# Near attention: the softmax weights are turned once per unit and repeated over the head's rows by DMA through DRAM

## The chip, the core and the metric

The kernel runs on one core of a Trainium2 chip. The metric is the device time of one execution, in microseconds; the profile's own clock, the span from the first to the last instruction, stands beside it. The core has five engines that work through their own instruction queues in order: TensorE (PE in the profile; PEld is its weight load), VectorE (DVE), ScalarE (ACT), GpSimd (POOL) and SyncE (SP, which here only issues DMA). ACT issues DMA too.

## The reference, cut to what matters

One layer of an encoder over 1024 tokens of width 1024. After an input layer norm, one projection makes the queries, keys and values of 24 attention heads (three groups of 8, with dilations 1, 4 and 16), the inputs of a bidirectional gated recurrence of 8 heads, and two merge gates. The change touches the end of the attention. Each group is a softmax over a window, and the three groups' outputs are mixed head by head with a softmax over their log-sum-exps:

```
def dilated_attention(aq, ak, av, slopes):
    for g, (window, dil) in enumerate(ATT_GROUPS):
        o, lse = dilated_group(aq[:, :, g], ak[:, :, g], av[:, :, g], window, dil, slopes[g])
    ...
    w = jax.nn.softmax(jnp.stack(lses), axis=0)
    o = jnp.sum(w[..., None] * jnp.stack(outs), axis=0)
```

Behind it come the output projections of attention and recurrence, the gated sum, two layer norms and a SwiGLU feed-forward layer.

## The kernel before, in words

**Stages.** Phase 1 makes the projection and, in between, the attention and the recurrence. Phase 2 merges them and applies the first norm, phase 3 is the feed-forward layer. Every float32 product is made of three matmuls on a rounded part and the rest ("hi" and "lo"): `mm3` (lines 272 to 274) issues hi x hi, hi x lo, lo x hi. The projection uses Winograd's form of Strassen's product: seven products over blocks of 128 columns, two column groups in turn, each product being 4 x 3 = 12 matmuls of 128x512 (a step, in what follows, is one of these matmuls). A product's weight block is loaded by SP (line 251, tiles `wa`), cut by a CAST on ACT (line 214, `w_hi`) and a subtraction on POOL (line 224, `w_lo`), three products ahead, in four buffers. ACT copies (line 726) and DVE adds (lines 572 to 599) bring the results out of the PSUM tiles `pj`; from there they go to DRAM (`hg..` for the recurrence, `at..` for attention).

**Units.** Between the steps of the projection's stream `phase1` runs side work, one unit at a time, written as a generator that gives way at each `yield`. There are 4 attention units (two of the 8 heads each, j = 0 to 3) in two parts, `att_far` (dilations 4 and 16) and `att_near` (dilation 1), and 8 recurrence heads (`hgrn_side`). A unit's inputs come from DRAM into ten slots of 128x1024 (`slot(n, ...)`), and its PSUM tiles are the four buffers `sd` (`ps_sd`). Behind each of the first three `att_near` stands a recurrence head. Its first t (slot 1) and second t (slot 3), q and hv are loaded by `fetch` (line 780); ACT turns t into the gate tiles fa and fb (lines 1149 to 1155), DVE scans them (line 1162), POOL multiplies t with fb (line 1170) and with their inverses (line 1183), and TensorE turns the result (line 1197). The tile fb of the head's first direction lies in slot 7, where the attention's result `ol` was.

**att_near, part by part.** `far` gives the far groups' result OL (128 rows: 64 for each of the two heads; 1024 tokens along the row) and their negative maxima N12 and sums L12. The scores of each 128 queries are made with the queries on partitions, with maximum, exp and sum (lines 1013 to 1030). Then both weights are worked out as tiles [128 queries, 2 heads, 8 query blocks], W0 for the near group and W12 for the far ones (lines 1035 to 1044). But OL and the near result have the head's rows on partitions and the queries along the row, so the weights must be turned, and each be repeated over the 64 rows of its head. Before, POOL first repeats every weight 64 times along the row (RB, two tiles of 128x1024, line 1048), and TensorE turns the 2 x 8 blocks of 128x128 (`spread`, line 1070), so that the repeated columns become repeated rows. The near weights are copied from PSUM to `near` (line 1075), the far ones stay in two PSUM tiles RL. The scores are turned as well (line 1062, 32 transposes), and 64 small matmuls with V give the near result in the two PSUM tiles O (line 1089). At the end OL = OL x RL + near x O (lines 1094 to 1098), stored by ACT (line 1099).

**What sets the order.** The kernel is built under a scheduler. It estimates each instruction's time, keeps the dependences, gives evacuations of `pj` a head start (`high_priority`), and fixes for each engine one order in which it then issues. The waits that are left are semaphores. Line numbers of the changed kernel are one higher above `att_near` and shift by a few inside it.

Of the kernel before, what the change touches and what calls it, by code (L numbers as in the profile page):

```python
# [10 lines left out]
F32 = mybir.dt.float32  # L11
# [9 lines left out]
T = 1024  # L21
KT = D // 128
HALF = 512
# [56 lines left out]
class Block:  # L80
    evac_ahead = 1000

    def __init__(self, ctx, tc, x, ln_in_g, ln_in_b, w_in, hgrn_lb, hgrn_norm_g, w_att_up, w_hgrn_up,
                 w_o, ln1_g, ln1_b, w_ffn_in, w_ffn_out, ln2_g, ln2_b, tabs, out, dbg=None):
        self.tc, self.nc, self.ctx = tc, tc.nc, ctx
        self.x = x[0]
        self.ln = {"in": (ln_in_g, ln_in_b), "1": (ln1_g[0], ln1_b[0]), "2": (ln2_g[0], ln2_b[0])}
        self.w_in, self.lbw, self.ng = w_in[0], hgrn_lb, hgrn_norm_g[0]
        self.wa, self.wr, self.wo = w_att_up[0], w_hgrn_up[0], w_o[0]
        self.wfi, self.wfo, self.tabs, self.out = w_ffn_in[0], w_ffn_out[0], tabs, out[0]  # L90
        self.dbg = dbg or {}
        nc = self.nc

        self.npj = 0
        self.issued = {}
        self.psum = ctx.enter_context(tc.tile_pool(name="psum", bufs=1, space=PSUM))
        self.cst = ctx.enter_context(tc.tile_pool(name="cst", bufs=1))
        self.tiny = ctx.enter_context(tc.tile_pool(name="tiny", bufs=1))
        self.spare = self.pad(self.cst, CST_PAD)
        self.wpool = self.pool("wp", "right")  # L100
        self.wp = self.wpool.__enter__()
        dram = ctx.enter_context(tc.tile_pool(name="dram", bufs=1, space=DRAM))

        def scratch(name, n):
            if name in self.dbg:
                return [self.dbg[name][i] for i in range(n)]
            return [dram.tile([128, 1024], F32, name=f"{name}{i}") for i in range(n)]

        self.att_d = scratch("att", 4)
        self.rec_d = scratch("rec", 8)  # L110
        self.tg_d = scratch("tg", 16)
        self.n1_d = scratch("n1", 8)
        self.ahs_d = scratch("ahs", 8)
        self.hg_d = [{n: dram.tile([128, T], F32, name=f"hg{h}{n}") for n in ("t0", "t1", "q", "v", "g")}
                     for h in range(8)]
        self.at_d = [{(k, g): dram.tile([128, T], F32, name=f"at{j}{k}{g}") for k in "qkv" for g in range(3)}
                     for j in range(4)]
        self.td = [dram.tile([128, 4, HALF], F32, name=f"td{i}") for i in range(3)]
        self.gd = {p: dram.tile([128, NF // 2, HALF], F32, name=f"gd{p}") for p in range(1, 8)}
        self.consts()  # L120
# [695 lines left out]
    HD = (slice(0, 64), slice(64, 128))  # L816
# [165 lines left out]
    def att_near(self, j, pre):  # L982


        nc, ident, HD, d = self.nc, self.ident, self.HD, self.at_d[j]
        OL, N12, L12 = self.far
# [45 lines left out]
                yield 2  # L1032
        V = self.turned(v.rearrange("p (k d) -> p k d", k=8), lambda kt: v[:, 128 * kt:128 * kt + 128])

        NM, W0, W12 = (self.att_small(n) for n in ("NM", "W0", "W12"))
        nc.vector.tensor_tensor(NM, N0, N12, OP.min)
        for w, n, l in ((W0, N0, L0), (W12, N12, L12)):
            nc.vector.tensor_sub(w, NM, n)
# [4 lines left out]
        for w in (W0, W12):  # L1043
            nc.vector.tensor_mul(w, w, L0)

        RB = [self.slot(1 + i, f"rb{i}", (8, 2, 64)) for i in range(2)]
        for r, w in zip(RB, (W12, W0)):
            nc.gpsimd.tensor_copy(r, w.rearrange("p a t -> p t a")[:, :, :, None].to_broadcast([128, 8, 2, 64]))
        yield 2

        kw = dict(skip_group_check=True)
# [4 lines left out]
        for b in range(4):  # L1056
            for hd in range(2):
                ps = self.ps_sd()
# [4 lines left out]
                self.copied(hd, P[b][:, hd].rearrange("p t c -> p (t c)"), ps)  # L1063
            if b % 2:
                yield b
        def spread(r):
            out = [self.ps_sd(), self.ps_sd()]
            for tt in range(8):
                c = 128 * (tt % 4)
                nc.tensor.transpose(out[tt // 4][:, c:c + 128], r[:, tt].rearrange("p a d -> p (a d)"), ident)  # L1070
            return out

        near = self.slot(2, "near")
        for b, ps in enumerate(spread(RB[1])):
            nc.scalar.copy(near[:, HALF * b:HALF * (b + 1)], ps)
        RL = spread(RB[0])
        O = [self.ps_sd(), self.ps_sd()]
        todo = []
        for kt in range(8):
            c = 128 * (kt % 4)  # L1080

            todo.append((kt, O[kt // 4], c + (64 if kt == 0 else 0), c + 128, kt, 192 if kt == 0 else 128))
            t = kt + 1
# [7 lines left out]
            begun.add(id(o))  # L1091
        cols = ((0, slice(64, 512), slice(0, 448)), (1, slice(0, 512), slice(448, 960)), (0, slice(0, 64), slice(960, 1024)))
        for b, src, dst in cols:
            nc.vector.tensor_mul(OL[:, dst], OL[:, dst], RL[b][:, src])
        for b, src, dst in cols:
            z = slice(HALF * b + src.start, HALF * b + src.stop)
            nc.vector.tensor_mul(near[:, z], near[:, z], O[b][:, src])
# [945 lines left out]
```

## Time and profile before

| | |
|---|---|
| median of 3 runs | 2035.15 us |
| lowest and highest run | 2034.71 and 2042.38 us |
| span of the profiled execution | 2034.2 us (its own device time is not shown beside it) |
| granted TensorE clock, mean | 0.998 |
| TensorE busy | 2005.5 us, 99% |
| DVE, ACT, POOL busy | 1310.3, 961.4 and 1026.6 us (64, 47 and 50%) |
| att_near, the part with `spread`, units 0 to 3 | starts at 344.8, 592.2, 840.6 and 1086.7 us |

The device time holds the span and what lies around it; the median stands 0.95 us above the span. A row of a timeline gives the start, the length in us, the engine, the line, the operation, "written tile <- read tiles", the shape, a count where equal neighbours are merged, and in brackets how long the engine stood idle before it and for whom. Matmuls overlap, so what one costs is read from the distance of starts and not from its length.

### The profile page before, as it was taken

The numbers are of one execution on the slowest core, as the hardware profiler recorded it, in microseconds if no ns is written. First come the engines' busy times: TensorE is split into PE (matmuls) and PEld (weight loads), VectorE is DVE, ScalarE is ACT, GpSimd is POOL, SyncE is SP. The second block draws the span as 40 slices with busy tenths as digits, with TensorE's granted clock in tenths as the row PEclk, the third lists the DMA queues.
The fourth block names the chain that finished last, engine by engine and source line by source line (L and its number), as shares of the span: only waits on it lengthen the run. The fifth ranks groups of instructions, "written<-read, shape, count | busy, mean of one in ns | idle before, by whom it ended". The sixth has DMA issues, their size and how long they took to land. (4 is left out here: it accounts for less than half of the span.)

```text
span 2034.2 us, 31011 instructions
## 1 busy us (share of the span) xinstructions
PE 2005.5 (99%) x11002; PEld 1666.0 (82%) x11002; DVE 1310.3 (64%) x2065; ACT 961.4 (47%) x1980; POOL 1026.6 (50%) x890
## 2 busy tenths in 40 slices
PE   7999999999999999999999999999999999999998
PEld 5788888788888888888888888888788888888886
DVE  7777545884458843778444226557776776767788
ACT  6654455554655535665465433244433333344541
POOL 6656644676446663466545662244765665630000
PEclk9999999999999999999999999999999999999999
DMA  5443533445333453343534477444434443447533
GB/s 160 153 137 120 174 118 109 132 135 171 119 123 125 135 170 104 125 141 125 170 99 149 132 258 234 143 144 141 139 135 140 135 140 130 129 168 288 165 98 126
DMA packets 274430, 296.93 MB, mean 146 GB/s; under 512 B 14113, under 2 KB 207458, under 8 KB 274274
## 3 DMA queue, kind: packets, MB, share of 16 engines
q1 hardware_dynamic: 267968, 273.73, 42.2%
q10 hardware_dynamic: 6306, 21.20, 2.7%
q8 instruction: 87, 1.43, 0.3%
q14 instruction: 69, 0.57, 0.1%
HBM read 200.77 MB, written 94.11 MB: 145 GB/s over the span
## 5 line engine op out<-in xcount | busy, mean ns | idle before, releaser
L224 POOL TENSOR_TENSOR w_lo<-wa,w_hi 128x512 fp32r<-128x512 f32 x272 | 364.4, 1349 | 273.5 <-ACT w_hi L214 235.0
L214 ACT CAST w_hi<-wa 128x512 fp32r<-128x512 f32 x272 | 168.7, 621 | 252.8 <-PE pj L273 151.5
L224 POOL TENSOR_TENSOR w_lo<-wsum,w_hi 128x512 fp32r<-128x512 f32 x88 | 127.9, 1464 | 111.1 <-PE sd L274 60.7
L224 POOL TENSOR_TENSOR w_lo<-f_raw,w_hi 128x512 fp32r<-128x512 f32 x66 | 101.2, 1540 | 51.5 <-ACT w_hi L214 50.3
L210 POOL TENSOR_TENSOR mv<-mv,mhalf 128x1 f32<-128x1 f32 x16 | 12.7, 792 | 221.7 <-DVE mv L209 218.6
L214 ACT CAST w_hi<-wsum 128x512 fp32r<-128x512 f32 x88 | 54.6, 621 | 116.7 <-PE sd L273 108.8
L214 ACT CAST gwsum<-a_raw 128x512 fp32r<-128x512 f32 (+1 forms) x78 | 48.2, 618 | 112.5 <-PE pj L273 54.1
L272 PE MATMUL pj<-xt1hi,w_hi 128*128 128x512 f32 x252 | 99.8, 396 | 0.0
L274 PE MATMUL pj<-xt1hi,w_lo 128*128 128x512 f32 x252 | 98.7, 392 | 0.0
L273 PE MATMUL pj<-xt1lo,w_hi 128*128 128x512 f32 x252 | 98.4, 391 | 0.0
L224 POOL TENSOR_TENSOR w_lo<-ws,w_hi 128x512 fp32r<-128x512 f32 x46 | 64.5, 1406 | 55.1 <-ACT w_hi L214 54.8
L583 DVE TENSOR_TENSOR evh<-wkeep,pj 128x512 f32<-128x512 f32 x45 | 30.8, 685 | 95.3 <-PE pj L274 55.5
L698 POOL TENSOR_TENSOR wa<-wa,wa 128x512 f32<-128x512 f32 x46 | 67.5, 1469 | 48.9 <-DVE wa L697 45.6
L572 DVE TENSOR_TENSOR evh<-wkeep,pj 128x512 f32<-128x512 f32 x66 | 58.0, 882 | 39.7 <-PE pj L274 29.4
L726 ACT COPY wkeep<-pj 128x512 f32<-128x512 f32 x136 | 79.4, 585 | 2.0 <-DVE evh L572 2.0
L274 PE MATMUL pj<-xt2hi,w_lo 128*128 128x512 f32 x192 | 75.8, 395 | 2.5 <-POOL w_lo L224 2.5
L273 PE MATMUL pj<-xt2lo,w_hi 128*128 128x512 f32 x192 | 75.5, 393 | 1.3 <-DVE xt2lo L404 1.3
L272 PE MATMUL pj<-xt2hi,w_hi 128*128 128x512 f32 x192 | 76.0, 396 | 0.7 <-ACT w_hi L214 0.7
L224 DVE TENSOR_TENSOR gwkeep<-a_raw,gwsum 128x512 fp32r<-128x512 f32 (+1 forms) x78 | 53.1, 680 | 36.5 <-ACT gwsum L214 33.7
L272 PE MATMUL pj<-xb11hi,w_hi 128*128 128x512 f32 x192 | 76.0, 398 | 0.4 <-DVE evh L583 0.4
L272 PE MATMUL pj<-xt4hi,w_hi 128*128 128x512 f32 x192 | 76.3, 397 | 0.0
L273 PE MATMUL pj<-xb11lo,w_hi 128*128 128x512 f32 x192 | 75.5, 394 | 0.0
(449 smaller groups left out, 6584.1 us busy)
## 6 DMA issues: line engine op xcount, KB each, us to landing
wa<-in_w_in_dram SPq DMA_DIRECT2D x184, 256.0 KB, 3.3
f_raw<-in_w_ffn_in_dram SPq DMA_DIRECT2D x44, 512.0 KB, 4.2
a_raw<-gd SPq DMA_DIRECT2D x30, 512.0 KB, 3.7
gd<-fc SPq DMA_DIRECT2D x44, 256.0 KB, 2.0
gd<-fs SPq DMA_DIRECT2D x33, 256.0 KB, 2.6
tg<-evh SPq DMA_DIRECT2D x32, 256.0 KB, 2.4
tg<-tg SPq DMA_DIRECT2D x16, 512.0 KB, 5.7
y<-ahs SPq DMA_DIRECT2D x16, 512.0 KB, 6.9
```

What stands on the lines that cost most here:

```text
L210: nc.gpsimd.tensor_tensor(mv[:, 2:3], mv[:, 2:3], self.mhalf[:, 0:1], OP.pow)
L214: ins = nc.scalar.copy(hi, src) if eng_hi == "act" else nc.vector.tensor_copy(hi, src)
L224: ins = e.tensor_sub(lo, src, hi.bitcast(F32))
L272: nc.tensor.matmul(ps, whi, xhi, start=first, stop=False, **kw)
L273: nc.tensor.matmul(ps, whi, xlo, start=False, stop=False, **kw)
L274: self.product = nc.tensor.matmul(ps, wlo, xhi, start=False, stop=last, **kw).ins.name
L572: self.left(nc.vector.tensor_tensor(o, self.order_src(add, g, kind), s, OP.add))
L583: self.left(nc.vector.tensor_add(t, add, ps))
L698: nc.gpsimd.tensor_sub(a["a21"], a["a22"], a["a11"])
L726: nc.scalar.copy(t, ps)
```

## The change

The two weights lie in one tile WW [128, 2 weights, 2 heads, 8 blocks]. One TensorE transpose makes of it 32 rows (weight, head, block) of 128 queries. ACT copies them to SBUF and stores them to a DRAM tile of 16 KB per unit. A head's 8 rows of one weight are, read on end, its 1024 queries; four DMA loads of SP (each 64 rows x 4 KB, all from the same 4 KB of DRAM) repeat them over the head's 64 rows in `near` (slot 2) and RL (slot 1). RL now is an SBUF tile, not two of PSUM, and the two POOL copies, 16 transposes and two ACT copies per unit are gone.

```diff
@@ att_near
+        WW = self.smt.tile([128, 2, 2, 8], F32, name="WW", tag="WW", bufs=1)
+        W0, W12 = WW[:, 0], WW[:, 1]
...
-        RB = [self.slot(1 + i, f"rb{i}", (8, 2, 64)) for i in range(2)]
-        for r, w in zip(RB, (W12, W0)):
-            nc.gpsimd.tensor_copy(r, w.rearrange("p a t -> p t a")[:, :, :, None].to_broadcast([128, 8, 2, 64]))
+        ps = self.ps_sd()
+        nc.tensor.transpose(ps[0:32, 0:128], WW.rearrange("p w a t -> p (w a t)"), ident)
+        wr = self.sm.tile([128, 128], F32, name="wrow", tag="xtmp", bufs=1)[0:32, :]
+        nc.scalar.copy(wr, ps[0:32, 0:128])
+        nc.scalar.dma_start(self.w_d[j], wr)
+        near, RL = self.slot(2, "near"), self.slot(1, "rl")
+        for w, t in enumerate((near, RL)):
+            for hd in range(2):
+                src = self.w_d[j][16 * w + 8 * hd:16 * w + 8 * hd + 8, :].rearrange("a b -> (a b)")
+                nc.sync.dma_start(t[HD[hd]], src[None, :].to_broadcast([64, T]))
         yield 2
...
-        def spread(r):
-            out = [self.ps_sd(), self.ps_sd()]
-            for tt in range(8):
-                c = 128 * (tt % 4)
-                nc.tensor.transpose(out[tt // 4][:, c:c + 128], r[:, tt].rearrange("p a d -> p (a d)"), ident)
-            return out
-
-        near = self.slot(2, "near")
-        for b, ps in enumerate(spread(RB[1])):
-            nc.scalar.copy(near[:, HALF * b:HALF * (b + 1)], ps)
-        RL = spread(RB[0])
...
-            nc.vector.tensor_mul(OL[:, dst], OL[:, dst], RL[b][:, src])
+            nc.vector.tensor_mul(OL[:, dst], OL[:, dst], RL[:, HALF * b + src.start:HALF * b + src.stop])
```

The scheduler's order changes with it. TensorE in unit 0, first before, where the weights (`rb_`) are turned between two steps of the projection:

```order
L274 MATMUL pj<-xt3hi,w_lo 128x512
L1070 MATMUL sd<-tabs_sb,rb_3471 128x128 x8
L1070 MATMUL sd<-tabs_sb,rb_3470 128x128 x8
L272 MATMUL pj<-xt3hi,w_hi 128x512
L273 MATMUL pj<-xt3lo,w_hi 128x512
```

And after at the same place, where the products with V now stand (before, they came 20 steps of the projection later):

```order
L275 MATMUL pj<-xt3hi,w_lo 128x512
L1088 MATMUL sd<-p_3287,v_3263 64x64 x2
L1088 MATMUL sd<-p_3287,v_3263 64x128 x4
L1088 MATMUL sd<-p_3311,v_3263 64x128 x8
L1088 MATMUL sd<-p_3374,v_3263 64x128 x8
L1088 MATMUL sd<-p_3390,v_3263 64x128 x8
L1088 MATMUL sd<-p_3287,v_3263 64x64 x2
L273 MATMUL pj<-xt3hi,w_hi 128x512
```

The new transpose stands three steps of the projection later than the first score transposes stood before, ahead of those, which are cut into groups of 12, 4, 12 and 4:

```order
L275 MATMUL pj<-xt2hi,w_lo 128x512
L1050 MATMUL sd<-tabs_sb,WW 32x128
L1072 MATMUL sd<-tabs_sb,p_3287 128x128 x8
L1072 MATMUL sd<-tabs_sb,p_3311 128x128 x4
L273 MATMUL pj<-xt2hi,w_hi 128x512
```

SP behind the weights of unit 0, first before, then after; `t_3713` and `t_3700` are the first t of the next recurrence head, `t_3717` and `t_3704` the second:

```order
L251 DMA wa_3608<-in_w_in_dram 128x4x128
L251 DMA wa_3628<-in_w_in_dram 128x4x128
L585 DMA hg3t_131<-evh 128x512
L780 DMA t_3713<-hg2t_125 128x1024
L251 DMA wa_3723<-in_w_in_dram 128x4x128
L573 DMA hg3v<-evh 128x512
L251 DMA wa_3744<-in_w_in_dram 128x4x128
L780 DMA hv<-hg2v 128x1024
L780 DMA q<-hg2q 128x1024
L780 DMA t_3717<-hg2t_126 128x1024
```

```order
L1058 DMA near<-wd_191 64x1024 x2
L1058 DMA rl<-wd_191 64x1024 x2
L252 DMA wa_3598<-in_w_in_dram 128x4x128
L781 DMA t_3700<-hg2t_125 128x1024
L252 DMA wa_3618<-in_w_in_dram 128x4x128
L252 DMA wa_3638<-in_w_in_dram 128x4x128
L586 DMA hg3t_131<-evh 128x512
L252 DMA wa_3710<-in_w_in_dram 128x4x128
L781 DMA hv<-hg2v 128x1024
L781 DMA q<-hg2q 128x1024
L781 DMA t_3704<-hg2t_126 128x1024
```

The first t moved from behind the store of `hg3t_131` to ahead of it and of two weight loads. ACT at the head behind unit 0, before and after; the conversions of `wa_3404` and `wa_3425` before are those of `wa_3408` and `wa_3429` after:

```order
L1149 ACTIVATE fa<-t_3713,gb,ga 128x8x63
L214 CAST w_hi<-wa_3404 128x512
L584 ACTIVATE evh<-evh 128x512
L1099 DMA att_71<-ol 128x1024
L214 CAST w_hi<-wa_3425 128x512
L1154 ACTIVATE fa<-t_3717,gb,ga 128x8x63
L1155 ACTIVATE fb<-t_3717,gb,ga 128x8x65
```

```order
L1098 DMA att_71<-ol 128x1024
L1153 ACTIVATE fa<-t_3704,gb,ga 128x8x63
L1154 ACTIVATE fb<-t_3704,gb,ga 128x8x65
L215 CAST w_hi<-wa_3408 128x512
L1149 ACTIVATE fb<-t_3700,gb,ga 128x8x65
L1156 ACTIVATE t_3704<-t_3704,ga,gna 128x1024
L585 ACTIVATE evh<-evh 128x512
L1156 ACTIVATE t_3700<-t_3700,ga,gna 128x1024
L215 CAST w_hi<-wa_3429 128x512
```

Both conversions moved from ahead of the second t's fa to behind it; on POOL the `w_lo` of `wa_3429` likewise moved behind both products of t with fb.

More of the change, by code (lines that the diff above doesn't have):

```diff
@@ L117, in __init__ @@
                      for j in range(4)]
+        self.w_d = [dram.tile([32, 128], F32, name=f"wd{j}") for j in range(4)]
         self.td = [dram.tile([128, 4, HALF], F32, name=f"td{i}") for i in range(3)]
@@ L1033, in att_near @@
         V = self.turned(v.rearrange("p (k d) -> p k d", k=8), lambda kt: v[:, 128 * kt:128 * kt + 128])
-        NM, W0, W12 = (self.att_small(n) for n in ("NM", "W0", "W12"))
+        NM = self.att_small("NM")
+        WW = self.smt.tile([128, 2, 2, 8], F32, name="WW", tag="WW", bufs=1)
+        W0, W12 = WW[:, 0], WW[:, 1]
         nc.vector.tensor_tensor(NM, N0, N12, OP.min)
```

## The prediction

> **What bounds the kernel now.** I read the engines' shares on the page first, then the waits of TensorE, then the timeline of one unit engine by engine, since a mean over the program would hide where the change sits.
>
> The page's span and the row of busy times:
>
> ```profile
> span 2034.2 us, 31011 instructions
> PE 2005.5 (99%) x11002; PEld 1666.0 (82%) x11002; DVE 1310.3 (64%) x2065; ACT 961.4 (47%) x1980; POOL 1026.6 (50%) x890
> ```
>
> TensorE is busy for all but 28.7 us; no other engine is near its limit. So a microsecond taken out of TensorE's own instructions is worth a microsecond, unless it comes back as a wait. TensorE's waits from 300 to 900 us, where the first three units and the recurrence heads behind them run (engine line, what it waited for, total us, times, longest):
>
> ```profile
> PE sd L1197 <- POOL t L1170: 1.8, 2, 1.2
> PE pj L274 <- POOL w_lo L224: 0.9, 1, 0.9
> PE pj L272 <- DVE evh L583: 0.4, 1, 0.4
> ```
>
> These are 3.1 us in 600 us. The side work (attention, recurrence) is written between the products of the big projection so that nobody waits for it, and the little waiting there is comes from the recurrence heads that follow each unit. The same heads are what this change moves.
>
> **What is removed.** The groups of the spread in the profile (line, engine, count, ns shortest/median/longest, first and last start):
>
> ```profile
> L1070 PE MATMUL sd<-tabs_sb,rb x64: 270/273/273, 344.8 to 1088.3; 128*128 128x128 f32 x64
> L1048 POOL COPY rb<-W x8: 1037/1042/1047, 329.8 to 1072.6; 128x1024 f32<-128x1024 f32 x8
> L1075 ACT COPY near<-sd x8: 567/590/604, 346.3 to 1088.3; 128x512 f32<-128x512 f32 x8
> ```
>
> The 273 ns is not the price of one transpose, since they overlap. The price is read from the starts around a group, here in unit 0 (start, us, engine, line):
>
> ```profile
> 330.37 1.91 PE L1062 MATMUL sd<-tabs_sb,p 128*128 128x128 f32 x16
> ...
> 344.55 0.39 PE L274 MATMUL pj<-xt3hi,w_lo 128*128 128x512 f32 x1
> 344.78 1.91 PE L1070 MATMUL sd<-tabs_sb,rb 128*128 128x128 f32 x16
> 346.44 0.48 PE L272 MATMUL pj<-xt3hi,w_hi 128*128 128x512 f32 x1
> 346.76 0.40 PE L273 MATMUL pj<-xt3lo,w_hi 128*128 128x512 f32 x1
> ...
> 363.81 0.39 PE L272 MATMUL pj<-xb11hi,w_hi 128*128 128x512 f32 x1
> ...
> 366.53 1.03 PE L789 MATMUL sd<-tabs_sb,hv 128*128 128x128 f32 x8
> 367.32 0.47 PE L272 MATMUL pj<-xb11hi,w_hi 128*128 128x512 f32 x1
> ```
>
> From 344.55 to 346.76 are 2.21 us; two product steps would take 2 x 0.227 (for example 363.81 lies 12 steps ahead of the transposes at 366.53, 2.72 us in all). The 16 transposes cost 2.21 - 0.45 = 1.76 us, 0.11 each. Four units: **-7.0 us** of TensorE. The POOL copies (8 x 1.04) and the ACT copies (8 x 0.59) lie on engines that are half idle: their removal is costed at nothing, and it only makes the halves of the weights (w_lo) a little earlier.
>
> **What is added on TensorE.** One transpose per unit, 32 rows out instead of 128. No row shows that shape; it lies between nothing and a full one, 0.11. I take the full one since the moving side is the same 128 columns: **+0.4 us** in all. That the score transposes now come in four groups and not two costs nothing: 16 cost 1.76, and 8 (at 366.53, followed 0.79 later) cost half.
>
> **What is added beside it.** Per unit a copy of 32x128 and a store issue on ACT, then four loads of 256 KB on SP; the store and two of the loads must land in turn before line 1093 can multiply. The nearest rows for the transfers, from the list of issues and from the rows of a repeated DRAM row (the two vectors that are spread over 128 partitions):
>
> ```profile
> gd<-fc SPq DMA_DIRECT2D x44, 256.0 KB, 2.0
> att<-ol ACTq DMA_DIRECT2D x4, 512.0 KB, 6.2
> L193 ACTq DMA_DIRECT2D ginb<-in_ln_in_g_dram x1: 339/339/339, 1170.5 to 1170.5; - x1
> L193 ACTq DMA_DIRECT2D binb<-in_ln_in_b_dram x1: 456/456/456, 1170.9 to 1170.9; - x1
> DMA to landing us min/median/max: 4.2/4.2/4.2
> ```
>
> The store of 16 KB lies between 2.0 and 6.2 us; I take 2.2, as it is nearest to the small one. The four loads are 1 MB from repeated rows, as the two vectors are: 4.2 us after issue, with 7.4 as the upper end (the t load below, third in a row of three).
>
> **Where it lands, walked through unit 0.** Rows of SP, ACT, DVE and POOL around it:
>
> ```profile
> 346.85 0.38 SPq L780 DMA_DIRECT2D t<-hg2t  x1
> 355.09 0.42 SPq L780 DMA_DIRECT2D t<-hg2t  x1
> 332.46 12.01 SPq L251 DMA_DIRECT2D wa<-in_w_in_dram  x6
> 331.48 0.59 ACT L726 COPY wkeep<-pj 128x512 f32<-128x512 f32 x1
> 357.25 0.63 ACT L584 ACTIVATE evh<-evh 128x512 f32<-128x512 f32 x1 [0.97 <-DVE evh L583]
> 351.04 0.81 ACT L1149 ACTIVATE fa<-t,gb,ga 128x504 f32<-128x504 f32 x1 [1.14 <-DMA t<-hg2t]
> 358.86 0.62 ACT L214 CAST w_hi<-wa 128x512 fp32r<-128x512 f32 x1 [0.98 <-PE pj L274]
> 362.52 0.81 ACT L1154 ACTIVATE fa<-t,gb,ga 128x504 f32<-128x504 f32 x1 [3.04 <-DMA t<-hg2t]
> 364.43 1.23 ACT L1157 ACTIVATE t<-t,ga,gna 128x1024 f32<-128x1024 f32 x1
> 345.04 0.69 DVE L583 TENSOR_TENSOR evh<-wkeep,pj 128x512 f32<-128x512 f32 x1 [6.85 <-PE pj L274]
> 346.29 1.35 DVE L1094 TENSOR_TENSOR ol<-ol,sd 128x448 f32<-128x448 f32 x3 [0.57 <-PE sd L1070]
> 358.42 1.75 DVE L1180 RECIPROCAL qd<-fa 128x256 f32<-128x256 f32 x1
> 363.36 1.23 DVE L1162 TENSOR_TENSOR_SCAN fa<-fa,d 128x512 f32<-128x512 f32 x1 [2.60 <-ACT fa L1154]
> 364.48 0.12 POOL L1148 MEMSET fb<- 128x8 f32 x1 [3.62 <-DMA att<-ol]
> 366.23 1.74 POOL L1170 TENSOR_TENSOR t<-t,fb 128x512 f32<-128x512 f32 x1
> 367.94 1.29 POOL L224 TENSOR_TENSOR w_lo<-wa,w_hi 128x512 fp32r<-128x512 f32 x1
> ```
>
> The new transpose stands three steps behind the old place of the score transposes, at 330.37 + 0.68 = 331.05. ACT copies it behind the row of 331.48, so at about 332.0, and issues the store at 332.3; it lands at 334.5. SP then issues near and rl by 335.8, and rl is there at about 340.5. SP stands still for the store meanwhile, but the six weight loads of that stretch went out over 12 us before, held by POOL and not by SP, so 2 us of standing still cost none of them much. DVE waits for rl with the three products of 1.35 until 341.8; behind them stands the evacuation that began at 345.04 before, so nothing is late. The t load in rl's slot waits for these products: out at 341.9 in place of 346.85, landed 4.2 later (351.04 - 346.85) at 346.1. So the trip through DRAM itself is covered, with some 3 us to spare against TensorE, which no longer reads the repeated weights at all.
>
> What is late next is the second t load. It stands on SP behind a store that needs this first one's scan (0.81 + 1.23 + 0.69 + 0.63 on ACT, DVE, DVE, ACT, to 349.5) and behind a weight load, hv and q: out at about 351.0 (355.09 before). With the 7.4 of before (to 362.52) it lands at 358.4. TensorE is 1.65 us earlier than before (1.76 - 0.11), so the gain of the load is 2.4 us against it. But the new order puts both fa and fb of this t *ahead* of the conversions (CAST) of two products, where it had stood behind both, and on POOL the second product's w_lo behind both products t x fb. The walk: fa and fb to 360.0, first CAST to 360.6; fb, t, evh and t (0.81 + 1.23 + 0.63 + 1.23) to 364.5, second CAST to 365.1. DVE: scan of fa to 360.4, evacuation 0.7, reciprocal 1.75, scan of fb to 364.1. POOL: t x fb 1.74 to 365.8, two small copies, t x fb again to 367.9, a small product, w_lo 1.29 to 369.3. TensorE asks for the first product at 363.81 - 1.65 = 362.2 (its w_lo is ready at about 362.3: tight) and for the second's w_lo with the third step behind 367.32 - 1.65: at 366.1. **It waits 3.2 us.** Before, the CAST of that product was done at 359.5, ahead of the late t.
>
> In units 1 and 2 one product, not two, goes behind the fa of the second t; I take half, 1.6 each, between nothing and 3.2. No head follows unit 3. New waits: 3.2 + 1.6 + 1.6 = **+6.4 us**. The 3.1 us of waits shown above belong to the same chains and are replaced: **-3.1**.
>
> The sum: 2034.2 - 7.0 + 0.4 + 6.4 - 3.1 = 2030.9 us of span. The time of this one execution is not shown beside its span; the median of the runs, 2035.15, lies 0.95 above, which I keep: **2031.9, said as 2032 us**.
>
> **A rule against the change.** The rows first: 512 KB to DRAM land in 6.2 us on ACT's queue, 256 KB in 2.0, and the t load in 7.4. The Trainium skill, page "DMA: Bandwidth & Descriptors", section "Anatomy of one DMA — SWDGE (gpsimd) path", puts about 2.0 us of fixed time on every transfer, most of it the receipt of the write, heaviest where DRAM is the target, plus bytes / 436e3 us. It speaks against a store followed by a load: two receipts. By it a t load behind two others (1.5 MB) would land in 5.6 us, the unit-0 wait would be 1.4, and the sum by this estimate about 2030. The trace's 7.4 does not agree, and the fit is of another issuing path, so the sum goes by the rows.
>
> **Rivals.**
> - *The saving stays whole.* If the t loads land as fast as the first one (4.2), the second is there at 355.2, 3.2 us sooner, and all new waits vanish: 2035.15 - 6.6 = 2028.5; if the old waits go too, 2025.4. For it: POOL is 8 x 1.04 us lighter around here. Against it: the 3.04 us that ACT stood before the second fa. Taken as 2027.
> - *Slower: the trip through DRAM decides.* If the store takes 6.2 and the loads 7.4, rl comes at 347.7 and not 340.5. The first t then goes out at 349, later than before; with slack already used, each of three heads holds TensorE up by up to 7.2 us more: 2032 + 21.6 = 2053. It turns into a loss when rl is about 1.1 us later than I say (3.2 us over three heads). Against it: near and rl go out when the trace has only weight loads.
> - *Nothing moves.* Waits eat the saving to the microsecond, if units 1 and 2 behave as unit 0: 2032 + 3.2 = 2035.
>
> **The numbers.** Forecast 0.50 (alone 2029 to 2034), saving whole 0.22, nothing moves 0.14, slower 0.14. Half a per cent, 10.2 us, is about what a measurement of this kernel can tell from no change: 2025.0 to 2045.3. Faster than that needs the first rival with all old waits gone and more, 0.04; slower needs the second rival's upper half, 0.07 of its 0.14; within it 0.89. The range of 8 in 10 leaves out the best tenth (under 2026) and the worst tenth (over 2040).
>
> **What would show it.** Right: 64 transposes gone and four small ones on TensorE; rl landed ahead of the fourth score copy's end plus 3 us; DVE idle before line 1093 for a DMA without an evacuation behind it being late; TensorE waiting for w_lo behind ACT's fa in units 0 to 2, some 2 to 7 us in all. Wrong: waits of TensorE on sd tiles of the unit itself (the new transpose waiting for its weights, or the products of V for a bank), the second t landing within 5 us, or SP's loads of weights late because near waits for the store.

## The result, and the profile after

The changed kernel takes 2041.63 us (median of 6 runs, 2039.87 to 2047.32), the kernel before in the same session 2035.03 (6 runs). The ratio is 1.0029, with a 95% interval of 1.0016 to 1.0043: about 6 us, or 0.3%, slower. That lies inside the half per cent that was called no change, but the sign is sure, and 2041.6 is outside the range of 2026 to 2040. The page of the profiled execution (2041.94 us, of which 2039.9 are its span):

```profile
span 2039.9 us, 30865 instructions
PE 2005.4 (98%) x10942; PEld 1662.7 (82%) x10942; DVE 1308.7 (64%) x2065; ACT 956.8 (47%) x1976; POOL 1015.5 (50%) x882
```

TensorE has 60 instructions less (64 transposes out, 4 in) and is busy for as long as before: it ran some of the others more slowly, as shown below. It also stood still for 34.5 us, where it was 28.7. The four new transposes, by line:

```profile
L1050 PE MATMUL sd<-tabs_sb,WW x4: 270/270/271, 332.6 to 1079.9; 128*32 128x128 f32 x4
```

TensorE's waits from 300 to 900 us, the view that showed 3.1 us before:

```profile
PE pj L273 <- ACT fb L1149: 4.0, 1, 4.0
PE pj L275 <- POOL w_lo L225: 2.8, 3, 1.6
PE pj L273 <- ACT wkeep L727: 1.3, 1, 1.3
PE sd L1305 <- DVE hon L1271: 0.3, 1, 0.3
PE sd L1196 <- POOL t L1182: 0.2, 1, 0.2
```

They are 8.6 us now. The wait of 4.0 us is that of a product's first step. The timeline of unit 0, the engines in the order SP, DVE, ACT, POOL (all of this execution runs 1.6 us later than the one before, from the start of the program on):

```profile
335.12 1.53 SPq L252 DMA_DIRECT2D wa<-in_w_in_dram  x3
336.76 1.17 SPq L1058 DMA_DIRECT2D near<-wd  x2
337.97 1.28 SPq L1058 DMA_DIRECT2D rl<-wd  x2
339.36 0.53 SPq L252 DMA_DIRECT2D wa<-in_w_in_dram  x1
347.96 0.34 SPq L781 DMA_DIRECT2D t<-hg2t  x1
357.04 0.43 SPq L781 DMA_DIRECT2D t<-hg2t  x1
346.57 1.36 DVE L1093 TENSOR_TENSOR ol<-ol,rl 128x448 f32<-128x448 f32 x3 [6.46 <-DMA rl<-wd]
366.05 1.23 DVE L1161 TENSOR_TENSOR_SCAN fa<-fa,d 128x512 f32<-128x512 f32 x1 [7.41 <-ACT fa L1153]
367.19 0.66 DVE L584 TENSOR_TENSOR evh<-wkeep,pj 128x512 f32<-128x512 f32 x1
351.77 0.81 ACT L1148 ACTIVATE fa<-t,gb,ga 128x504 f32<-128x504 f32 x1 [6.83 <-DMA t<-hg2t]
365.21 0.81 ACT L1153 ACTIVATE fa<-t,gb,ga 128x504 f32<-128x504 f32 x1 [9.62 <-DMA t<-hg2t]
366.64 0.60 ACT L215 CAST w_hi<-wa 128x512 fp32r<-128x512 f32 x1
370.66 0.60 ACT L215 CAST w_hi<-wa 128x512 fp32r<-128x512 f32 x1
374.76 1.26 POOL L225 TENSOR_TENSOR w_lo<-wa,w_hi 128x512 fp32r<-128x512 f32 x1
```

Read in the order of time, the chain is this. The loads of rl go out at 338; DVE, idle for 6.46 us, starts its products at 346.57; only then SP can issue the first t (347.96), and the second follows at 357.04. It lands 8.1 us later. ACT, idle for 9.62 us, does its fa and fb ahead of the product's conversion (366.64), and DVE does its scan (366.05) ahead of the evacuation that frees a bank for the product (line 584). TensorE needs both. The view of waits names `fb`, the operation of ACT behind the conversion, but the conversion was over at 367.24 and the evacuation at 367.85; TensorE began at 368.00. So the evacuation ended this wait. The same 0.15 us lie between the two in every kernel below that has this wait, and in one of them (rl_t1_first) the view names the evacuation itself. The wait behind it, 1.57 us at 376.08, is for the next product's w_lo (374.76), which stands on POOL behind both products of t with fb. The list of transfers from 333 to 346 us (KB each, median us from issue to landing) shows why rl was late:

```profile
wa<-in_w_in_dram SPq DMA_DIRECT2D x4, 256.0 KB, 5.4
near<-wd SPq DMA_DIRECT2D x2, 256.0 KB, 6.4
rl<-wd SPq DMA_DIRECT2D x2, 256.0 KB, 7.4
wd<-wrow ACTq DMA_DIRECT2D x1, 16.0 KB, 1.8
```

The store was quick (1.8 us). But three weight loads (335.12) stand directly ahead of near and rl and one (339.36) behind: 2 MB in one queue within 5 us, and each of the loads whose landing the trace tells took longer than the one ahead of it. What the late t cost TensorE (rows of TensorE, then the granted clock in windows; columns of the second: window, us, busy, clock, DMA share, GB/s):

```profile
363.58 0.39 PE L275 MATMUL pj<-xt4hi,w_lo 128*128 128x512 f32 x1
368.00 0.47 PE L273 MATMUL pj<-xb11hi,w_hi 128*128 128x512 f32 x1 [4.04 <-ACT fb L1149]
...
370.56 0.63 PE L273 MATMUL pj<-xb11hi,w_hi 128*128 128x512 f32 x1
370.99 0.63 PE L274 MATMUL pj<-xb11lo,w_hi 128*128 128x512 f32 x1
...
372.81 1.04 PE L790 MATMUL sd<-tabs_sb,hv 128*128 128x128 f32 x8
...
376.08 0.50 PE L275 MATMUL pj<-xb11hi,w_lo 128*128 128x512 f32 x1 [1.57 <-POOL w_lo L225]
```

```profile
368.00:372.00 4.00, 3.88 (x10) 0.62 0.18 66
862.00:866.00 4.00, 3.04 (x9) 0.74 0.16 56
```

Behind the wait the granted clock falls to 0.62, and a step takes 0.43 us (370.99 - 370.56) where it takes 0.227. The twelve steps from 368.00 to 372.81 take 4.81 us and not 2.72: 2.1 us that no row of waits shows. It happens once more, in unit 2 (0.74 at 862). This comes out of the time that TensorE would otherwise have stood still, as the end of the next part shows.

**How kernels are compared here.** Times of single executions scatter by several us. In the traces, one of each kernel and two of the changed one, a large part of the differences lies in the program's start: the same instructions reach the 1000th product step (128x512), ahead of unit 0, up to 5.3 us apart. TensorE issues as many product steps in every kernel, so I take the start times of the steps number 1000, 1400, 2100, 2900 and 3700 from each trace; they enclose units 0 to 3. The table gives what each stretch grew against the kernel before (negative is faster), "ahead" being the delay at step 1000. The last column is the start of fa of the second t behind unit 0 on ACT, less "ahead" (362.52 in the kernel before). Each kernel's ratio is to the kernel before in its own session.

| kernel | ratio of the times (95%) | ahead | unit 0 | unit 1 | unit 2 | unit 3 | units | late t, us |
|---|---|---|---|---|---|---|---|---|
| changed | 1.0029 (1.0016 to 1.0043) | 1.57 | 4.19 | -0.93 | 2.11 | -1.13 | **4.2** | 363.64 |
| changed, again | one run | 2.17 | 4.45 | -1.20 | 2.28 | -1.55 | **4.0** | 363.91 |
| no_loads6 | 0.9978 (0.9965 to 0.9990) | 0.60 | -2.36 | -2.42 | 0.10 | -1.57 | **-6.3** | 357.05 |
| rl_slot6 | 1.0018 (1.0007 to 1.0030) | 5.28 | 2.07 | 1.67 | -0.15 | -1.08 | **2.5** | 361.42 |
| rl_first | 1.0013 (1.0005 to 1.0022) | 5.13 | 4.15 | -2.39 | 1.04 | -1.57 | **1.2** | 363.59 |
| fa_behind | 1.0013 (1.0004 to 1.0022) | 3.88 | 2.76 | -1.02 | 1.97 | -1.57 | **2.1** | 363.92 |
| early_loads | 1.0009 (0.9999 to 1.0018) | 1.88 | -2.07 | -2.42 | 3.65 | 0.60 | **-0.2** | 357.35 |
| rl_t1_first | 1.0011 (1.0000 to 1.0022) | 1.59 | 4.51 | -2.49 | -0.17 | -0.99 | **0.9** | 362.09 |
| hybrid | 0.9991 (0.9981 to 1.0001) | 3.12 | -2.60 | -1.52 | -0.12 | -0.65 | **-4.9** | 356.76 |
| hybrid_rl | 1.0040 (1.0028 to 1.0052) | 4.74 | 2.47 | 0.84 | 2.53 | -0.65 | **5.2** | 361.87 |
| wd_inside | 1.0018 (1.0010 to 1.0027) | 0.55 | 4.28 | -0.99 | 1.30 | -1.57 | **3.0** | 363.72 |
| hybrid_inside | 0.9981 (0.9972 to 0.9990) | 0.52 | -2.74 | -1.50 | -0.50 | -0.42 | **-5.2** | 356.66 |
| before_wd | 1.0016 (1.0006 to 1.0025) | 4.76 | -0.73 | -0.78 | 1.70 | 0.00 | **0.2** | 362.11 |
| before_store | 1.0008 (0.9999 to 1.0017) | 3.01 | -0.22 | -0.44 | 0.72 | 0.00 | **0.1** | 362.62 |
| before_wd_last | 1.0016 (1.0007 to 1.0025) | 4.57 | -0.87 | -0.78 | 2.31 | 0.00 | **0.7** | 361.97 |

Behind unit 3 nothing changes by more than 0.4 us in any kernel. The changed kernel's 5.7 us of span are 1.6 ahead of the units and 4.2 in them.

**What the last column says.** In the ten profiles from changed to hybrid_inside, leaving out fa_behind and rl_t1_first, which reorder ACT behind this t, unit 0 is the late t's start less 359.4, to 0.1 us (363.64 gives 4.2, 356.66 gives -2.7). From that start to the last step that waits (376.08 in the changed kernel) it is 10.85 to 10.92 us in all ten. In four of them the clock falls in between (changed, again, rl_first, wd_inside), in six it does not. So in the kernels with this order the loss behind unit 0 follows the second t's arrival, us for us, and the slow steps cost nothing of their own: with the clock up, TensorE would have stood still instead.

Unit 2 is another case. There the changed kernel's second t starts at 857.6 us and the kernel before's at 858.7, both less "ahead", so it is no later. But from that fa to TensorE's turn of line 1196 (1197 before) it is 16.57 us and not 12.55. This is the new order's doing: no_loads6, without any loads, has the same 16.58. Here too the clock costs nothing, for the second execution of the changed kernel keeps its clock in unit 2 and has 16.58 as well.

### The profile page after: what moved, and what is told of

Same layout as the page of the kernel before. It is cut to its first block, busy times and chain, and to the rows that moved or that the text cites. A ratio compares the mean times of both kernels' runs of the same rounds, so it can differ in the third digit from the quotient of the medians.

```text
span 2039.9 us, 30865 instructions
## 1 busy us (share of the span) xinstructions
PE 2005.4 (98%) x10942; PEld 1662.7 (82%) x10942; DVE 1308.7 (64%) x2065; ACT 956.8 (47%) x1976; POOL 1015.5 (50%) x882
## 5 line engine op out<-in xcount | busy, mean ns | idle before, releaser
L275 PE MATMUL pj<-xb11hi,w_lo 128*128 128x512 f32 x192 | 75.9, 396 | 1.7 <-POOL w_lo L225 1.6
```

Source lines behind the costliest of these rows:

```text
L275: self.product = nc.tensor.matmul(ps, wlo, xhi, start=False, stop=last, **kw).ins.name
```

## The experiments

The theory after the result (A): the transposes' time is really saved, but rl lands late in unit 0, the first and second t queue up behind it, ACT does the late t ahead of conversions, and TensorE's waits with a fallen clock eat the saving. Rivals: the order alone costs (B), the bytes of the loads cost (C).

**No loads.** `for t in (near, RL): nc.gpsimd.memset(t, 0.5)` in place of the four loads, and `RL = self.slot(6, "rl")`.

> The changed kernel without its four loads per unit: near and rl are filled with a constant by two POOL MEMSETs instead (so the output does not hold the weights); rl lies in slot 6, so that no t load waits for it; the small transpose and the store stay, and TensorE's order of instructions is the changed kernel's. Theory A (the 64 transposes are worth 6.6 us, and the late loads give it back): units 0 to 2 lose their new waits, 2035 - 6.6 = 2028.5, at most 2031 with the second t still ahead of the conversions on ACT. Rival B (taking the transposes out is worth nothing here, or the new order on ACT and POOL alone makes the waits, whatever the loads do): 2035 to 2042.

The median is 2032.22 us (before 2036.24 in the same runs), the units give -6.3. That is above the 2031 of theory A, though the session was 1.2 us slower for the kernel before, too. The saving that I put at 6.6 (7.0 - 0.4) is there, in an order of TensorE that is the changed kernel's but for a few groups in units 1 and 2 that stand up to six product steps away. Of the waits from 300 to 1140 us two are left that count:

```profile
PE sd L1196 <- POOL t L1169: 1.6, 1, 1.6
PE pj L275 <- POOL w_lo L225: 1.5, 1, 1.5
```

So the loads and what hangs on them cost 4.2 + 6.3 = 10.5 us. Rival B in its first form falls as the account of the whole; the wait of 1.6 us for line 1169, in unit 2, is the order's.

**rl in another slot.**

```diff
-        near, RL = self.slot(2, "near"), self.slot(1, "rl")
+        near, RL = self.slot(2, "near"), self.slot(6, "rl")
```

> The changed kernel with one number changed: rl lies in slot 6 (empty in this unit) and not in slot 1, which the first t load needs; that load moves on SP from behind the loads of rl to ahead of the unit's weight loads. All transfers stay. Theory A (rl lands some 5 us later than I said, and the first t, the store behind its scan and the second t queue up behind it): the first fa starts as soon as the products with rl are done, about 348.5 in place of 351.8, the second t goes out some 3 us sooner, and 2 to 4 us of the waits of units 0 and 2 go: 2036 to 2039. Rival B (order alone): 2041 to 2042. Rival C (the transfers themselves, through the bandwidth they take): 2041 to 2042, with the t loads still landing after 8 us.

2042.43 us against 2036.24, above A's range; the profile has 5.28 us of delay ahead of the units, and the units cost 2.5 in place of 4.2. The load of the first t waits for nothing now, yet the fa of this t writes slot 6 and so still waits for DVE's products with rl, and the second t gains 3 us (352.3 against 355.5, both less their start). The big wait breaks into smaller ones (300 to 560 us):

```profile
PE pj L273 <- ACT fb L1149: 1.9, 1, 1.9
PE pj L275 <- POOL w_lo L225: 1.6, 1, 1.6
PE pj L273 <- DVE evh L600: 1.5, 1, 1.5
```

and behind these the granted clock stays at 1.00. Units 0 and 2 together gain 4.4 us, what A said and a little more. Unit 1 came out 2.6 us worse than in the changed kernel; two waits of 0.7 and 1.3 us there, which begin 1.4 us apart, were again followed by a fall of the clock (0.57 from 622 to 626 us).

**rl ahead of near.** `for w, t in ((1, RL), (0, near)):`

> The changed kernel with the two loads of rl issued ahead of the two of near. Theory A (rl is late since it stands behind near): rl is issued 1.2 us sooner and shares the engines with nothing ahead of it: landed 2 to 3 us sooner, line 1093 starts at 343.5 to 344.5 in place of 346.6, and half of the loss in units 0 and 2 goes: 2037 to 2040. Rival D (each repeated load takes its 5 to 7 us whatever stands ahead): 1.2 us sooner, 2040 to 2041. Rival B (order alone): 2041.6.

2040.10 us against 2036.24, the units 1.2. DVE's products in unit 0, and the loads there (336 to 352 us; this execution is 5.1 us late from the start):

```profile
348.38 1.36 DVE L1093 TENSOR_TENSOR ol<-ol,rl 128x448 f32<-128x448 f32 x3 [7.98 <-DMA rl<-wd]
```

```profile
rl<-wd SPq DMA_DIRECT2D x2, 256.0 KB, 7.0
near<-wd SPq DMA_DIRECT2D x2, 256.0 KB, 7.8
```

Less the 5.1 that is 343.2, 1.8 us sooner than in the changed kernel (345.0), though nothing of near stands ahead any more: the weight loads do. That is nearer D than A in unit 0, whose loss stays (4.15): the second t goes out 1.1 us sooner than in the changed kernel and lands 9.2 us later, so it comes no sooner. In units 1 and 2, with fewer loads beside it, the same edit gives 1.5 and 1.1 us.

**Conversion ahead of the late t.** The fa and fb of head 2's second t: `self.behind(fa1, self.cast)`, `self.behind(fb1, self.cast)`.

> The changed kernel with the fa and fb of the second t of head 2 held behind the next conversion (CAST) on ACT; SP's order is unchanged, and so are all transfers; only unit 0 is touched. Theory A with the order as the second half of the mechanism: the wait of 4.0 us of the first product behind unit 0 (TensorE line 273, released by ACT fb) goes, of which 1 to 2 us come back at the next product: 2038 to 2040. Rival E (the conversion is late for another reason, such as its weights): 2041.6, and the wait stays under another name.

2038.63 us against 2036.24, inside A's range; unit 0 at 2.76 in place of 4.2, but not in the way expected. The first wait is gone, and with it went more than the edit names: the scheduler's new order puts DVE's evacuation of line 584 ahead of the late scan, too (361.00, the scan at 368.64). A wait of 4.7 us stands at the next product, where 1 to 2 were expected (300 to 560 us):

```profile
PE pj L273 <- DVE evh L600: 4.7, 1, 4.7
```

There DVE has the late t (its scans of fa and fb) ahead of the next evacuation that frees a bank. A step put ahead moves the wait to the next one behind the late t: the lateness is the cause, the place of the wait is not.

**The same bytes, early.**

```diff
-                src = self.w_d[j][16 * w + 8 * hd:16 * w + 8 * hd + 8, :].rearrange("a b -> (a b)")
-                nc.sync.dma_start(t[HD[hd]], src[None, :].to_broadcast([64, T]))
+                src = self.at_d[j]["q", 0][2 * w + hd:2 * w + hd + 1, :]
+                nc.sync.dma_start(t[HD[hd]], src.to_broadcast([64, T]))
```

> The changed kernel whose four loads per unit read rows of a q table that has lain in DRAM for long, instead of the stored weights (so the output does not hold the weights): as many transfers of the same size and shape, each DRAM row repeated over 64 partitions, but they go out ahead of the unit, some 15 us sooner; rl stays in slot 1, the transpose and the store stay. Theory A (the loss is that rl comes late): as without loads, 2030 to 2033, and TensorE gains 5 to 6.5 us over the four units. Rival C (the loss is the megabyte itself, which at the 330 GB/s seen around 340 us takes 3.2 us from the weight and t loads of each unit): 2036 to 2041, TensorE gains nothing over the units.

2038.49 us against 2035.98, and -0.2 over the units: by both sums this is what C said and not A. The single units tell more. Units 0 and 1 gain 2.07 and 2.42, nearly the same as without loads (2.36 and 2.42): sent early, the megabyte costs nothing there. That a megabyte next to the t loads costs nothing is not shown by this. Units 2 and 3 lose, by a wait of their own (300 to 1140 us):

```profile
PE sd L1050 <- DVE WW L1047: 1.9, 1, 1.9
```

The products with rl now stand early on DVE (824.20 in unit 2, after 2.25 us of waiting for rl), and WW, which comes behind them there, is late. Neither theory had that.

**The second t ahead of q.** rl first, and in `hgrn_pre`: `for s, n in ((3, "t1"), (1, "t0"), (0, "q"))`.

> The changed kernel with rl loaded ahead of near and, in the recurrence heads, the second t ahead of the first t and q in the program (on SP it moves one place, ahead of q's 512 KB). Theory A: the second t of head 2 lands 1.5 to 2 us sooner, the wait behind unit 0 shrinks from 4.1 to about 2.4 us, under which the granted clock does not fall (in the changed kernel it fell to 0.62 behind that wait), which spares 2 us more: 3 to 4 us less than with rl first alone, 2034.5 to 2036.5. Rival F (hv ahead of it fills the queue; one place changes nothing): 2038 to 2039.

2038.82 us against 2035.98: not A's 3 to 4 us, and inside F's range. Yet F's reason is not what happened. The second t does come 1.5 us sooner than with rl first alone (362.09 against 363.59), as A had it. But the scheduler's order changed as well: ACT now does three operations on this t (fa, fb and the t of line 1156) ahead of the conversion, and from fa to the last step that waits it is 12.1 us, where it was 10.9. So unit 0 stays at 4.5. The first of its waits (300 to 560 us):

```profile
PE pj L273 <- DVE evh L584: 3.6, 1, 3.6
```

Behind it the granted clock is 0.50 (370 to 374 us). Of the units only unit 2 gained.

**The changed kernel again.** The same file.

> The changed kernel once more, unedited. If the differences of a few us between the kernels are theirs, its TensorE start times from the first unit to the end of the fourth repeat those of the first profile to 0.5 us (the step over the four units is +4.2 us against the kernel before), and only the stretch ahead of the units, the same program in all these kernels, differs, by 0 to 5 us. If units differ by over 1 us from run to run, single profiles can't carry the account.

The units repeat to 0.4 us each and 0.3 in the sum (4.0 against 4.2); the stretch ahead of them is 0.6 longer. So a trace's steps repeat. But the table's three last rows show unit 2 moving by 0.7 to 2.3 us, and the others by up to 0.9, where only a store and, in two of them, unread tables were added: a single stretch that differs by less than 2 us proves little, and the verdicts go by sums and by larger steps.

**Half the change: near through DRAM, rl by transposes.**

```diff
-        near = self.slot(2, "near")
-        for b, ps in enumerate(spread(RB[1])):
-            nc.scalar.copy(near[:, HALF * b:HALF * (b + 1)], ps)
-        RL = spread(RB[0])
+        RL = spread(r)
```

with W0 alone turned, stored (8 KB) and loaded twice as in the change.

> Half of the change: near, wanted last, comes through DRAM (one transpose to 16 rows, a store of 8 KB, two loads); rl, wanted first, is still spread by eight transposes per unit into PSUM, so that nothing on DVE or in slot 1 waits for a transfer. 32 transposes less, 4 more. Theory A: the saving is 3.5 - 0.4 = 3.1 us and no new wait comes: 2032 to 2034, against 2036 for the kernel before in the same runs. Rival C (bytes): half a megabyte per unit delays the second t by 1.6 us in three units: 2036 to 2039. Rival B (any new order costs): 2036 to 2040.

The median is 2035.24 us against 2035.98 (ratio 0.9991, not told apart from no change), above A's range. The units give -4.9 us, more than the 3.1 of the transposes: the old waits went too. TensorE's waits from 300 to 1140 us, and the second t at ACT (this execution is 3.1 us late from the start):

```profile
PE pj L275 <- POOL w_lo L225: 0.7, 2, 0.4
PE sd L1312 <- DVE hon L1278: 0.4, 1, 0.4
PE sd L1203 <- POOL t L1189: 0.3, 1, 0.3
```

```profile
359.88 0.81 ACT L1160 ACTIVATE fa<-t,gb,ga 128x504 f32<-128x504 f32 x1 [3.86 <-DMA t<-hg2t]
360.59 0.82 ACT L1161 ACTIVATE fb<-t,gb,ga 128x520 f32<-128x520 f32 x1
361.31 0.60 ACT L215 CAST w_hi<-wa 128x512 fp32r<-128x512 f32 x1
```

The order on ACT is the changed kernel's, fa and fb ahead of the conversion. But the t is there at 356.8 (359.88 - 3.1) and not at 363.6, and nobody waits. So behind unit 0 this order costs nothing as long as the t is early. In unit 2 the hybrid's order is not the changed kernel's (12.8 us from fa to the turn of t, not 16.6), so it says nothing of that unit. Of the 4.9 us only 0.7 came through in the median; the profile has 3.1 of delay ahead of the units.

**The other half: rl through DRAM, near by transposes.** The same with the weights exchanged.

> The other half of the change: rl, wanted first and lying in the slot of the first t, comes through DRAM; near is still spread by eight transposes per unit. As many transposes and bytes as in the first half. Theory A (lateness of what is wanted first): rl lands at 341 to 343 us in unit 0 and not ahead of the first t's turn at 346.8 minus its products, the second t is ahead of the conversions again, and the units cost TensorE +0 to +4 us, against -4.9 for the other half: 2037 to 2041. Rival C (bytes): the same as the other half, 2035.

2046.10 us (5 runs) against 2036.53, above A's range; the units cost 5.2 where the first half gives 4.9. As many transposes and bytes, and 10 us between them: C, the bytes alone, falls. But A's way to it was not this. rl landed early, with half the bytes (rows of the loads, 336 to 352 us, and the timeline; 4.7 us late from the start):

```profile
rl<-wd SPq DMA_DIRECT2D x2, 256.0 KB, 5.3
```

```profile
345.56 1.78 DVE L1102 TENSOR_TENSOR ol<-ol,rl 128x448 f32<-128x448 f32 x3 [5.29 <-DMA rl<-wd]
347.80 6.78 SPq L252 DMA_DIRECT2D wa<-in_w_in_dram  x2
357.04 0.42 SPq L781 DMA_DIRECT2D t<-hg2t  x1
366.61 0.81 ACT L1162 ACTIVATE fa<-t,gb,ga 128x504 f32<-128x504 f32 x1 [8.95 <-DMA t<-hg2t]
```

That is 340.8, just when the prediction has it. Yet the second t went out at 352.3, because SP stood 6.78 us in two weight loads whose buffers came free late (they waited for POOL's w_lo, 5.9 us the longer time), and it then landed 9.5 us after issue, behind hv, q and a weight load.

**Where the start loses time.** Three edits: the stored weights inside an existing DRAM table, `self.w_d = [self.n1_d[j][0:4, :].rearrange("a (b c) -> (a b) c", c=128) for j in range(4)]`, in the changed kernel (wd_inside) and in the half change (hybrid_inside); and the kernel before with the added tables and one store of a constant per unit (before_wd).

> The changed kernel with the stored weights put into the first four rows of DRAM tables that exist anyway and are free at that time, so that the program has no DRAM table more than before; the orders of all engines are the changed kernel's. Account so far: every kernel with the added table came 1.5 to 4 us later by its median than its TensorE steps over the four units say, all of it ahead of the units, in code that the change does not touch. Theory G (the added table shifts what lies behind it, and the loads at the start pay): about 2 us less than the changed kernel, 2039 to 2040, the start as in the kernel before. Rival (the start differs by chance, or for another reason): 2041 to 2042. Over the four units TensorE loses 4.0 to 4.5 us by either.

> The half change (near through DRAM, rl by transposes) with its stored weights in an existing DRAM table. Theory G: the 4.9 us that TensorE gained over the units come through whole: 2030.5 to 2032.5. Rival: as the half change, 2034 to 2036.

> The kernel before with the four DRAM tables of the change added and one store of 16 KB into them per unit (of a constant, used by nobody); nothing else. Theory G: 1.5 to 2.5 us slower than the kernel before, all of it at the start, 2037.5 to 2038.5; the units as before, to 0.3 us. Rival: no difference.

wd_inside: 2040.71 us against 2036.53, between the two expectations; its units make 3.0 of it, less than either theory said, and the interval overlaps the changed kernel's, so this alone decides nothing. hybrid_inside: 2032.46 us against 2036.53, ratio 0.9981 (0.9972 to 0.9990), 0.2% faster than the kernel before, with a span of 2029.7 us.

before_wd: 2040.46 us against 2036.53, slower by 3 to 4 us with nothing changed in the units' sum (0.2, though unit 2 moved by 1.7); all 4.8 of its profile stand ahead of them. That is more than G said, and at the start, as G said. For G's reason, that the tables shift what lies behind them, the stores were tried without added tables, and with the tables behind all others:

> The kernel before with one store of 16 KB per unit into rows of a DRAM table that exists anyway (of a constant, used by nobody until the table is written over): the stores of the last test without its added tables. Theory G (the added tables shift what lies behind them): as the kernel before, 2035.5 to 2037. Rival H (the program with the stores, however placed, starts later): 2038.5 to 2041, as with the tables.

> The same stores into four added DRAM tables that are laid out behind all others. Theory G: as the kernel before, 2035.5 to 2037, since nothing moves. Rival H: 2038.5 to 2041. Rival I (an added table costs wherever it lies, for instance through the number of tables): 2038.5 to 2041 here, but not with the stores alone.

The stores alone: 2037.49 against 2036.75, ratio 1.0008, not told apart from no change. The tables behind all others: 2040.31, ratio 1.0016, as slow as in the first place. So G's reason falls. I fits, but it is not shown: the interval of the stores alone (0.9999 to 1.0017) overlaps that of the tables (1.0007 to 1.0025). Over all kernels, the median's distance to the kernel before, less the units, is 1.9 to 4.4 us in ten of the eleven with added tables (fa_behind 0.3) and 0.6 to 1.2 in the three without. Single traces do not separate them: the stores alone have 3.0 ahead, five profiles with the tables 0.6 to 2.2. Why is open; in the traces the extra stands in waits for the first loads and conversions within the first 160 us.

## Why the prediction was wrong, step by step

- *Removed, -7.0, and added, +0.4.* Right. Without the loads the units gain 6.3 us with 0.7 more of waits left than before. In unit 1 the new transpose and twelve others cost 1.34 us and twelve alone 1.22, so it is worth about the 0.11 that I took.
- *The store, 2.2 us.* Right: 1.8.
- *"rl is there at about 340.5."* This is the step that failed. The landing was taken as 4.2 us, from two loads with little beside them, with 7.4 as the upper end (335.8 + 4.2 is 340.0 and not 340.5, a slip that changes nothing). It was 7.4 for the first load of rl, the second was issued 0.7 us behind it, and DVE began at 345.0 (346.57 - 1.57), 4.5 late. The weight loads that I counted as spread over 12 us went out as three in a row directly ahead. In units 1 and 2 the loads of near and rl, with no weight load directly ahead, took 3.5 to 5.5; rl with three weight loads but not near ahead of it (rl_first) took 7.0. So the upper end goes with a full queue, and the walk did not count what stands in it.
- *"The trip through DRAM itself is covered."* It followed from that step and fell with it. Everything behind moved by the same 4.5 us: first t 346.4 (341.9 said), second t 355.5 (351.0).
- *Landing of the second t, 7.4.* 8.1 here, 9.5 with half the loads: too small by 0.7 here. Its fa began at 363.6, 5.2 later than said. hybrid_rl shows that rl on time was not enough: there the second t went out late for another reason, and landed later still.
- *Unit 0 waits 3.2.* The walk behind the late t was right: from its fa (358.4) to the second product's w_lo (369.3) it has 10.9 us, and the trace has 10.87 from fa to the step that waits for w_lo. Only its start was wrong. With the t 5.2 later the walk gives 3.2 + 5.2 = 8.4 us for TensorE; it lost 8.1 (4.0 ahead of 368.00, and 8.08 in place of 4.06 us from there to 376.08). The slow steps that the walk did not have are part of that. For the first product the walk looked at the w_lo (362.3); DVE's evacuation, by its figures at 361.1, ended that wait.
- *Units 1 and 2, 1.6 each.* This is the second term that failed. They were taken as half of unit 0 without a walk of their own. The waits are 1.0 and 2.0 us, and in unit 2 eight steps from 863.9 to 867.4 us take 3.5 us and not 1.8. Unit 2 lost 2.1 us, with a t that was no later than before: the new order makes the way from it to TensorE 4.0 us longer.
- *Old waits, -3.1.* Gone as said in the first profile; in the second execution one of 1.6 us for POOL's t stands in unit 2. Against no_loads6, step by step, TensorE stands still 5.1 us longer and its steps and side work take 5.4 us longer, nearly all of it in the slow steps and at restarts behind waits. That is the 10.5 us.
- *Ahead of the units, 0.* 1.6 in the profile; the two kernels that add only unread tables and stores are slower by 3.6 and 3.9 us in the median. No row of before could show that.
- *The time is 0.95 above the span.* In every run with both figures it is 1.7 to 2.4, here 2.0. So the profiled execution, 2041.94, lies 10.1 above the forecast: 7.5 in the units (-3.3 said, 4.2 measured), 1.6 ahead of them, 1.0 here.

The rivals: the slower one, that the trip through DRAM decides, is what happened behind unit 0, and its turning point of 1.1 us was passed (rl was 4.5 late). Its upper figure of 2053 was too high, since only unit 0 had the full queue. The Trainium skill's rule in "DMA: Bandwidth & Descriptors", "Anatomy of one DMA — SWDGE (gpsimd) path", 2.0 us and the bytes at 436 GB/s, would by estimate give 2.6 us for each of these loads, which go out on another issuing path. They took 3.5 to 7.4, so the trace does not agree.

## What to carry to other kernels

Do not take a transfer's time from its like with little beside it: count the bytes that go out within a few us around it, and take the upper bound where the path is then the longest. Then follow the latest arrival to its end: here TensorE's loss behind unit 0 grew, us for us, with the arrival of one load, and slow steps on the way were no loss of their own. Which weight goes through DRAM made 10 us of difference for the same transposes and bytes (near, wanted last, -5; rl, wanted first, +5). That what is wanted first should stay on the engines is suggested by this pair and not shown, for in the second kernel rl came in time and SP's order made the loss. And an order that a scheduler changes along the way needs a walk for every unit, not for the first alone.

## What the runs showed of the hardware

**The clock.** One idle time of 4.0 us brought steps of 0.427 us in place of 0.227 for about 4 us. The Trainium skill, "TensorE: Matmul & The Clock Gate", Part 1, has the clock at half after an idle window of about 3.4 us; with that unit 0 agrees. Unit 2 does not: two waits of 1.3 and 0.8 us, which begin 2.2 us apart, were enough for 0.74 in the window behind them. Yet the same program, run again, kept 1.00 there (862 to 866 us) through the same two waits of 1.4 and 0.8 us. The kernel before kept its clock through two waits of 1.2 and 0.9 us that begin 3.4 us apart (376 to 384 us):

```profile
376.00:380.00 4.00, 2.83 (x17) 1.00 0.00 0
380.00:384.00 4.00, 3.10 (x14) 1.00 0.00 0
```

and rl_slot6 through three of 1.5 to 1.9 us within 10. So the lengths of the waits alone do not decide it; no run here shows what does.

**The start.** The same instructions ahead of unit 0 took up to 5.3 us longer from one program to the next (0.6 between two executions of the same), and with four added DRAM tables that nobody reads and a store into each the median moved by 3.6 to 3.9 us (before_wd, before_wd_last). That the tables and not the stores do it is likely and not shown. Differences of a few us between programs need the trace, or a count of what stands ahead of the edit.
